# Block 0's V rows in two PSUM banks from the last recall on, and GpSimd for the lower parts of the weights from there

## The chip, the cores and the metric

The kernel runs on one core of a Trainium2 chip. The metric is the device time of one execution in microseconds (us). The engines are named as the profile names them: PE (TensorE matmul), PEld (its weight load), DVE (VectorE), ACT (ScalarE), POOL (GpSimd) and SP (SyncE, which issues most DMAs).

## The reference

One decoder layer on 512 tokens of width 1024. Three token mixers (forgetting attention, a sliding window, attention over a memory) each have a projection; sigmoid gates merge them and an output projection adds the sum to `x`. Then 8 heads choose 16 of 16384 one-neuron experts per token, so each token has 128 rows of `u` and 128 rows of `v`.

```
h = RMSNorm(x);  z = h @ w_in                     # q, k, v of the mixers, memory queries, three gates
merged = g0*(o_fox @ w_fox_o) + g1*(o_swa @ w_swa_o) + g2*(o_mem @ w_mem_o)
x = x + merged @ w_out
h2 = RMSNorm(x); experts, gates = top-16 per head by product keys
a = dot(h2, u[expert]);  x = x + sum_e gelu(a_e) * gate_e * v[expert_e]
```

## The kernel before

The 512 tokens are 4 blocks of 128 (one token per partition). `mixers(g, hT)` runs twice: for group 0 (block 0 alone) and for group 1 (blocks 1, 2 and 3 together, 384 tokens). Blocks 0 and 1 fetch their expert rows with GpSimd's indirect DMAs, one row of 1024 floats per token and expert; blocks 2 and 3 later multiply with all experts densely.

**Weights in two parts.** Matmuls are made exact by splitting: `load` (from L115) fetches a tile of 128 x 1024 into `raw` (SP's queue), ACT casts it into `whi` (L119), and `rest` (L122) makes the lower part `wlo = raw - whi`. `rest` adds its argument `pool` to a counter `due`; when that reaches 1, GpSimd makes this lower part (L129), else VectorE does (L131). `load_split` passes `share[0]` unless told otherwise. `raw`, `whi` and `wlo` have three buffers each. `mm3` (L145 to L147) multiplies three times per pair of parts, and two of the three need only `whi`.

**Rows beside the mixers.** While group 1 mixes, a generator `beside` works for block 0: the search for its experts, their choice, and then the rows. `pump` is called at each weight tile and each attention head, adds credit and lets the generator run. `step` (from L858) issues the gathers up to four rows ahead (L868, five buffers `row`) and uses the next one: a U row with a multiply that sums (L883, into `acts`), a V row with a multiply-add. As long as the list `two` is empty, a V row of block 0 is added to `x1[0]`, a tile `mg` in SBUF (L890: row, factor, `mg` in, `mg` out). Once `two` holds a tile of two PSUM banks, the first row of a block starts that sum (L893) and each further row is added to it there (L896). After a block's last row, `two` is added to `x1`. A step with `apart` goes another way: ACT scales the row (L886) and GpSimd adds it to `x1` in SBUF (L887). `beside` stops when 183 of block 0's 256 rows are done (128 U rows and 55 V rows).

**The end of group 1's mixers.** After the last `recall` (attention over the memory, L555 to L577, which sums in the bank `acc`) come `gates(1, 2)` with 8 weight tiles, `branch(1, 2)` with 4 (L604 and L605 gate and merge each product), the split of `merged` (L661, L662) and the output projection with 8 weight tiles (L673 adds `x`). These 20 tiles, 128 x 1024 each, have their lower parts made at L131, since `beside` set `share[0]` to 0 when it came to the rows. Then the pool `mixed` (banks `tg` and `acc`) is closed, `two` is opened in its place (L961 and L962), `x1` is normalized and turned (L239), and the search for blocks 1 to 3 begins.

**What sets the order.** Up to that search the framework's scheduler orders each engine's instructions ahead of time, by a priority that is the order in the program; the rows are pushed back by 400 places (`high_priority(-LATER)`). The order on each engine is then fixed: an instruction that waits holds all behind it on its engine. The dense part after the search is ordered by hand.

Of the kernel before, what the change touches and what calls it, by code (L numbers as in the profile page):

```python
# [7 lines left out]
F32 = mybir.dt.float32  # L8
# [8 lines left out]
S, D, NB, KC = 512, 1024, 4, 8  # L17
# [5 lines left out]
NJ = PH * TOPK  # L23
# [34 lines left out]
def tile_block(ctx: ExitStack, tc: tile.TileContext, t: dict, out: bass.AP):  # L58
# [12 lines left out]
    mixing, two = ExitStack(), []  # L71
    mixed = mixing.enter_context(tc.tile_pool(name="mixed", bufs=1, space=bass.MemoryType.PSUM))

    def bank(tag):
        return (mixed if BANKS[tag] == 1 else psum).tile([128, 512], F32, tag=tag, name=tag, bufs=BANKS[tag])
# [4 lines left out]
    def pump(part=1.0):  # L80
        if inside[0]:
            return
        inside[0] = True
        credit[0] += part * PACE[pace[0]]
        while credit[0] > 0:
            if pace[0] == "search":
                cost = next(side[0], None)
            else:
                with tc.high_priority(-LATER):
                    cost = next(side[0], None)  # L90
            if cost is None:
                credit[0] = 0.0
                break
            credit[0] -= cost
        inside[0] = False


    due, share = [0.0], [0.0]
# [50 lines left out]
    def small_f(n, tag, bufs=None):  # L149
        return small.tile([128, n], F32, tag=tag, name=tag, **({"bufs": bufs} if bufs else {}))  # L150
# [9 lines left out]
    def by_k(x):  # L160
        return x.rearrange("p (k s) -> p k s", k=KC)
# [156 lines left out]
    def halves(two):  # L318

        return two[:, :, :512], two[:, :, 512:]  # L320

    def gemm_tr(h, src):

        w = load_split(src, 8, 128)
        ps = bank("mm")[:, :h[0][0].shape[1]]
        for dc in range(KC):
            mm3(ps, (w[0][:, dc], w[1][:, dc]), (h[0][dc], h[1][dc]), dc == 0, dc == KC - 1)
        return ps
# [41 lines left out]
    def p_t(p, tiles):  # L370
        ps = bank("tp")
        for i in range(tiles):
            PE.transpose(ps[:, i * 128:(i + 1) * 128], p[:, i * 128:(i + 1) * 128], ident)
        pT = pp.tile([128, 512], F32, tag="pT", name="pT")
        A.copy(pT[:, :tiles * 128], ps[:, :tiles * 128])
        return pT

    def new_p():
        return pp.tile([128, 512], F32, tag="p", name="p")
# [5 lines left out]
    def finish(oT, po, den, nh, hd, i0, lb):  # L385

        w = nh * hd
        V.reciprocal(den, den)
        o = pp.tile([128, 512], F32, tag="o", name="o", bufs=1)
        V.tensor_mul(o[:, :w].rearrange("p (h d) -> p h d", h=nh), po[:, :w].rearrange("p (h d) -> p h d", h=nh),  # L390
                     den[:, :, None].to_broadcast([128, nh, hd]))
        ps = bank("tp")
        for i in range(w // 128):
            PE.transpose(ps[:, i * 128:(i + 1) * 128], o[:, i * 128:(i + 1) * 128], ident)
        dst = slice(i0, i0 + w // 128), slice(lb * 128, (lb + 1) * 128)
        split(oT[0][:, dst[0], dst[1]], oT[1][:, dst[0], dst[1]], ps[:, :w].rearrange("p (u t) -> p u t", t=128))
# [158 lines left out]
    def recall(g, qT, oT):  # L555
        for lb in range(len(GROUPS[g])):
            po, den = bank("acc"), small_f(4, "fden")
            for i in range(2):
                pump(0.5)
                sc = bank("sc").rearrange("p (g k) -> p g k", g=2)  # L560
                nm, p = small_f(2, "nm"), new_p()
                for j in range(2):
                    PE.matmul(sc[:, j], qT[:, 2 * i + j, lb * 128:(lb + 1) * 128], mkT[:, 2 * i + j, :],
                              start=True, stop=True)
                V.tensor_reduce(nm, sc, axis=AX.X, op=OP.max, negate=True)
                for j in range(2):
                    A.activation(p[:, j * 256:(j + 1) * 256], sc[:, j], AF.Exp, bias=nm[:, j:j + 1],
                                 accum_out=den[:, 2 * i + j:2 * i + j + 1])
                pT = p_t(p, 4)
                for j in range(2):  # L570
                    h = 2 * i + j
                    for k in range(2):
                        PE.matmul(po[:, h * 128:(h + 1) * 128], pT[:, (2 * j + k) * 128:(2 * j + k + 1) * 128],
                                  mv[:, k, h * 128:(h + 1) * 128], start=k == 0, stop=k == 1)
            finish(oT, po, den, 4, 128, 0, lb)


    def new_g(w):
        return pp.tile([128, BIG * 128], F32, tag="g", name="g", bufs=KC)[:, :w]

    def gates(g, i, hT, ccs=range(4)):
        gs = []
        for cc in ccs:
            c0 = 8 * i + 2 * cc
            if len(GROUPS[g]) == 1:
                bias = pp.tile([128, 256], F32, tag="sq", name="bias")
                for c in range(2):
                    A.activation(bias[:, c * 128:(c + 1) * 128], ident, AF.Copy, scale=hb[:, c0 + c:c0 + c + 1])
                gs.append(new_g(256))
                gemm_nat(hT, halves(t["w_tr"][c0:c0 + 2]), 256, 1,  # L590
                         lambda b, ps: A.activation(gs[-1], ps, AF.Tanh, scale=0.5), more=bias)
                continue
            for c in range(2):
                ps = gemm_tr(hT, t["w_tr"][c0 + c])
                gs.append(new_g(ps.shape[1]))
                A.activation(gs[-1], ps, AF.Tanh, bias=hbh[:, c0 + c:c0 + c + 1], scale=0.5)
        return gs

    def branch(grp, i, merged, oT, gs):
# [7 lines left out]
        for cc in range(4):  # L607
# [7 lines left out]
            for c in range(2):  # L615
# [4 lines left out]
                        kc == 0, kc == 3)  # L620
                gated(by_k(merged)[:, 2 * cc + c], gs[2 * cc + c], ps)

    def mixers(g, hT):

        nb = len(GROUPS[g])
        skvf(g, hT)
        oT = new_oT(g)
        qT = fox_qkv(g, 0, hT)
        if g == 0:
            memory()  # L630
            biases()
        fox(g, 0, qT, oT)
        qT = fox_qkv(g, 1, hT)
        fox(g, 1, qT, oT)
        merged = wide(f"mg{g}", nb)
        gs = gates(g, 0, hT)
        qT = window_q(g, hT)
        branch(g, 0, merged, oT, gs)
        oT = new_oT(g)
        window(g, qT, oT)  # L640
        gs = gates(g, 1, hT)
        qT = memory_q(g, hT)
        branch(g, 1, merged, oT, gs)
        oT = new_oT(g)
        recall(g, qT, oT)
        gs = gates(g, 2, hT)
        if g == 0:
            get_x()
        branch(g, 2, merged, oT, gs)

        mT = [by_k(ep.tile([128, D], F32, tag="own", name="own"))] if nb == 1 else pair(nb)
        if nb == 1:
            for q in range(2):
                ps = bank("tp")
                for i in range(4):
                    PE.transpose(ps[:, i * 128:(i + 1) * 128], merged[:, (4 * q + i) * 128:(4 * q + i + 1) * 128], ident)
                ps, dst = ps.rearrange("p (k s) -> p k s", k=4), slice(4 * q, 4 * q + 4)
                A.activation(mT[0][:, dst], ps, AF.Copy, scale=0.5)
        else:
            for ct, src in enumerate(chunks(by_k(merged))):  # L660
                A.activation(mT[0][:, ct], src, AF.Copy, scale=0.5)  # L661
                V.scalar_tensor_tensor(mT[1][:, ct], src, 0.5, mT[0][:, ct].bitcast(F32),  # L662
                                       op0=OP.mult, op1=OP.subtract)
        mT = [chunks(x) for x in mT]
        x1, sums = by_token(wide(f"mg{g}", nb)), new_sums(4)
        for c in range(4):
            xs = [new_g(256) for _ in range(nb)]
            cols = slice(c * 256, c * 256 + 256)
            for lb, b in enumerate(GROUPS[g]):
                nc.sync.dma_start(xs[lb], t["x"][b * 128:(b + 1) * 128, cols])  # L670

            def use(b, ps):
                V.tensor_add(x1[:, b, cols], xs[b], ps)  # L673
                squares(x1[:, b, cols], sums[:, b, c:c + 1])

            if nb == 1:
                gemm_plain(mT[0], t["w_out"][c], 256, use, load_raw)
            else:
                gemm_nat(mT, t["w_out"][c], 256, nb, use)
        return x1, sums  # L680
# [174 lines left out]
    known, issued, done, ahead, flying, rpool = [2 * NJ], [0], [0], [AHEAD], {}, []  # L855
# [102 lines left out]
    share[0] = 0.5  # L958
    xb, sums = mixers(1, hT)
    side[0] = iter(())  # L960
    mixing.close()  # L961
    two.append(ctx.enter_context(tc.tile_pool(name="two", bufs=1, space=bass.MemoryType.PSUM)).tile([128, D], F32, name="two"))  # L962
    for lb, b in enumerate(GROUPS[1]):
        x1[b] = xb[:, lb]
    pre.close()
# [390 lines left out]
```

## Time and profile before

| what | value |
|---|---|
| median of 3 runs | 1589.84 us (1589.75 to 5559.83) |
| profiled execution, its own time | 1593.83 us |
| its span in the profile | 1592.1 us |
| mean granted TensorE clock | 0.982 |
| busy share: PE, PEld, DVE, ACT, POOL | 95, 86, 90, 52, 49 % |

The profile shows one execution. Its page gives busy time per engine and groups of instructions by line; further views of the same trace give the groups of one stretch, what an engine waited for, the chain of work that ended last, and the instructions in order of time. PE is the engine with the largest share, but a share is a mean over stages, so a stage has to be looked at by itself. The time of the profiled execution is 4.0 us above the median.

### The profile page before, as it was taken

The numbers are of one execution on the slowest core, as the hardware profiler recorded it, in microseconds if no ns is written. First come the engines' busy times: TensorE is split into PE (matmuls) and PEld (weight loads), VectorE is DVE, ScalarE is ACT, GpSimd is POOL, SyncE is SP. The second block draws the span as 40 slices with busy tenths as digits, with TensorE's granted clock in tenths as the row PEclk, the third lists the DMA queues.
The fourth block names the chain that finished last, engine by engine and source line by source line (L and its number), as shares of the span: only waits on it lengthen the run. The fifth ranks groups of instructions, "written<-read, shape, count | busy, mean of one in ns | idle before, by whom it ended". The sixth has DMA issues, their size and how long they took to land.

```text
span 1592.1 us, 27209 instructions
## 1 busy us (share of the span) xinstructions
PE 1514.5 (95%) x9458; PEld 1374.6 (86%) x9458; DVE 1433.5 (90%) x2666; ACT 829.5 (52%) x1840; POOL 779.0 (49%) x639
## 2 busy tenths in 40 slices
PE   8999899999999989999995999899999999999998
PEld 7989799997888988999885898788888888888887
DVE  6678477989899999999899999799999999999998
ACT  7778336646345534454215998554454444454443
POOL 1100015768576455467744665455555454555451
PEclk9999999999999999999997999999999999999999
DMA  8677657898899899965897999999999999999995
GB/s 328 222 236 249 242 182 247 316 357 299 314 346 322 273 348 346 382 217 185 290 411 247 380 393 392 344 399 390 409 410 410 409 411 409 395 409 411 410 409 213
DMA packets 178361, 531.90 MB, mean 334 GB/s; under 512 B 17456, under 2 KB 46384, under 8 KB 178224
## 3 DMA queue, kind: packets, MB, share of 16 engines
q0 software_dynamic: 73728, 268.47, 44.8%
q1 hardware_dynamic: 94416, 225.95, 38.9%
q10 hardware_dynamic: 10080, 35.75, 5.6%
q8 instruction: 74, 1.21, 0.3%
q14 instruction: 63, 0.52, 0.1%
HBM read 515.42 MB, written 14.68 MB: 333 GB/s over the span
## 4 chain that ended last, share of the span: by engine, by line
PE 54%; DVE 13%; issue 12%; DMA 11%; POOL 6%; ACT 4%; DVEq 0%; POOLq 0%; SPq 0%; ACTq 0%
PE mm L146 8%; PE mm L1029 8%; PE mm L147 8%; PE mm L145 8%; DMA row<-in_peer_v_dram,eidx 5%; POOL row L868 4%; DMA row<-in_peer_u_dram,eidx 4%; DVE wlo L131 3%; PE sc L1103 3%; DVE two L896 2%; PE sc L146 1%; PE sc L147 1%; PE sc L145 1%; PE tp L145 1%; PE tp L146 1%
## 5 line engine op out<-in xcount | busy, mean ns | idle before, releaser
L868 POOL DMA_INDIRECT row<-in_peer_v_dram,eidx x256 | 320.9, 1254 | 287.1 <-DVE two L896 162.8
L868 POOL DMA_INDIRECT row<-in_peer_u_dram,eidx x256 | 318.2, 1243 | 237.2 <-DVE scr L883 135.0
L131 DVE TENSOR_TENSOR wlo<-raw,whi 128x1024 fp32r<-128x1024 f32 (+1 forms) x244 | 304.2, 1248 | 33.6 <-ACT whi L119 26.5
L896 DVE SCALAR_TENSOR_TENSOR two<-row,acts,two 128x1024 f32<-128x1024 f32 x176 | 226.2, 1285 | 3.4 <-DMA row<-in_peer_v_dram,eidx 1.1
L119 ACT CAST whi<-raw 128x1024 fp32r<-128x1024 f32 x146 | 152.6, 1050 | 100.4 <-PE mm L146 62.4
L883 DVE SCALAR_TENSOR_TENSOR scr<-row,own 128x1024 bf16<-128x1024 f32 x128 | 156.3, 1221 | 22.2 <-DMA row<-in_peer_u_dram,eidx 21.2
L883 DVE SCALAR_TENSOR_TENSOR scr<-row,two 128x1024 bf16<-128x1024 f32 x117 | 142.2, 1216 | 6.0 <-DMA row<-in_peer_u_dram,eidx 5.0
L203 POOL TENSOR_TENSOR rsy<-rsv,mhalf 128x4 f32<-128x4 f32 (+5 forms) x25 | 39.9, 1600 | 184.3 <-DVE rsv L202 130.5
L1156 ACT CAST ah<-ga 128x256 fp32r<-128x256 f32 x116 | 47.1, 407 | 156.3 <-PE tp L146 118.4
L145 PE MATMUL mm<-hhi,whi 128*128 128x384 f32 x320 | 110.1, 344 | 1.2 <-DVE mg L673 0.7
L1158 ACT CAST whi<-raw 128x1024 fp32r<-128x1024 f32 x96 | 100.4, 1048 | 18.2 <-DMA raw<-in_peer_v_dram 12.7
L146 PE MATMUL mm<-hlo,whi 128*128 128x384 f32 x320 | 109.7, 343 | 0.0
L147 PE MATMUL mm<-hhi,wlo 128*128 128x384 f32 x320 | 108.9, 340 | 0.0
L146 PE MATMUL sc<-wlo,ah 128*128 128x512 f32 x256 | 101.4, 396 | 6.3 <-DVE wlo L131 6.3
L145 PE MATMUL mm<-whi,hhi 128*128 128x256 f32 (+1 forms) x360 | 103.7, 290 | 2.9 <-DVE g L604 1.9
L146 PE MATMUL mm<-wlo,hhi 128*128 128x256 f32 (+1 forms) x360 | 102.6, 286 | 1.7 <-DVE wlo L131 1.6
L147 PE MATMUL mm<-whi,hlo 128*128 128x256 f32 (+1 forms) x360 | 101.9, 285 | 0.8 <-DVE hlo L662 0.8
L147 PE MATMUL sc<-whi,al 128*128 128x512 f32 x256 | 101.8, 398 | 0.0
L145 PE MATMUL sc<-whi,ah 128*128 128x512 f32 x256 | 101.3, 396 | 0.2 <-ACT whi L1158 0.2
L145 PE MATMUL tp<-whi,ah 128*128 128x512 f32 x256 | 101.1, 395 | 0.0
L146 PE MATMUL tp<-wlo,ah 128*128 128x512 f32 x256 | 100.8, 394 | 0.0
L147 PE MATMUL tp<-whi,al 128*128 128x512 f32 x256 | 100.7, 393 | 0.0
(322 smaller groups left out, 4544.9 us busy)
## 6 DMA issues: line engine op xcount, KB each, us to landing
raw<-in_peer_v_dram SPq DMA_DIRECT2D x96, 512.0 KB
hhi<-in_uT_dram ACTq DMA_DIRECT2D x68, 512.0 KB
raw<-in_w_tr_dram SPq DMA_DIRECT2D x48, 512.0 KB
raw<-in_w_nat_dram SPq DMA_DIRECT2D x40, 512.0 KB
last<-in_peer_v_dram SPq DMA_DIRECT2D x32, 512.0 KB
hhi<-in_uT_dram SPq DMA_DIRECT2D x26, 512.0 KB
raw<-in_w_o_dram SPq DMA_DIRECT2D x24, 512.0 KB
gd<-st SPq DMA_DIRECT2D x24, 512.0 KB
```

The source lines that it names most:

```text
L119: (cast or A.copy)(hi[:, :n * w], raw[:, :n * w])
L131: V.tensor_sub(lo, raw, hi.bitcast(F32))
L145: PE.matmul(ps, lh, rh, start=first, stop=False)
L146: PE.matmul(ps, lh, rl, start=False, stop=False)
L147: PE.matmul(ps, ll, rh, start=False, stop=last)
L868: G.indirect_dma_start(out=r, out_offset=None, in_=t["peer_" + tab], in_offset=bass.IndirectOffsetOnAxis(ap=eidx[b][:, j:j + 1], axis=0))
L883: V.scalar_tensor_tensor(scr, r, 1.0, two[0] if b else h2n[b], op0=OP.mult, op1=OP.mult, accum_out=acts[b][:, c]))
L896: V.scalar_tensor_tensor(two[0], r, acts[b][:, c], two[0], op0=OP.mult, op1=OP.add))
L1029: PE.matmul(ps[:, :TD], w[:, dc], h2f[dc], start=dc == 0, stop=dc == KC - 1)
L1103: PE.matmul(ps[:, u], o[:, 1, u], o[:, 0, u], start=True, stop=True)
L1156: A.copy(ah, a)
L1158: A.copy(hi, raw)
```

## The change

`rows_in_psum` is new: it closes the pool `mixed`, opens the two banks as `two` and sets `share[0]` to 1, so that each later `load_split` of group 1's mixers hands its lower part to GpSimd. `mixers` calls it for group 1 right after the last `recall`. The two lines that closed `mixed` and opened `two` after the mixers are gone. `share[0]` goes back to 0 ahead of the last search, as before. From L623 on line numbers are up to 9 higher in the changed kernel (L868 is L877, L890 is L899, L893 is L902, L896 is L905).

```diff
+    def rows_in_psum():
+        mixing.close()
+        pool = ctx.enter_context(tc.tile_pool(name="two", bufs=1, space=bass.MemoryType.PSUM))
+        two.append(pool.tile([128, D], F32, name="two"))
+        assert done[0] >= NJ
+        share[0] = 1.0
+
     def mixers(g, hT):
...
         oT = new_oT(g)
         recall(g, qT, oT)
+        if g:
+            rows_in_psum()
         gs = gates(g, 2, hT)
...
     side[0] = iter(())
-    mixing.close()
-    two.append(ctx.enter_context(tc.tile_pool(name="two", bufs=1, space=bass.MemoryType.PSUM)).tile([128, D], F32, name="two"))
```

Two places show how the built orders differ. The first is POOL's order from the first V row's gather on, the stretch in which the 20 lower parts are needed (`row` is a row buffer, `eidx` the chosen experts, `wlo` a lower part). Before:

```order
L868 DMA row<-in_peer_u_dram,eidx_206 128x1024 x6
L868 DMA row<-in_peer_v_dram,eidx_206 128x1024 x52
L203 TENSOR_TENSOR rsy<-rsv,mhalf 128x3
L868 DMA row<-in_peer_v_dram,eidx_206 128x1024 x6
L722 TENSOR_TENSOR cand<-v_7904 128x3x24
```

Now, the start of the same stretch:

```order
L877 DMA row<-in_peer_v_dram,eidx_206 128x1024
L129 TENSOR_TENSOR wlo<-raw,whi 128x1024
L877 DMA row<-in_peer_v_dram,eidx_206 128x1024 x3
L129 TENSOR_TENSOR wlo<-raw,whi 128x1024
L877 DMA row<-in_peer_v_dram,eidx_206 128x1024 x2
L129 TENSOR_TENSOR wlo<-raw,whi 128x1024
L877 DMA row<-in_peer_v_dram,eidx_206 128x1024 x3
L129 TENSOR_TENSOR wlo<-raw,whi 128x1024
```

So it goes on for all 20: one to four gathers stand ahead of each lower part, 45 gathers from the first lower part to the last.

The second place is DVE's order where `x1` is turned, at the end of the mixers (`mg_2288` is `x1[0]` in SBUF, `hlo<-tp` the turn of `x1`). Before:

```order
L239 SCALAR_TENSOR_TENSOR hlo<-sc,gcol,hhi 128x384
L890 SCALAR_TENSOR_TENSOR mg_2288<-row,acts_207,mg_2288 128x1024
L1044 COPY rstd<-rsy 128x3
L890 SCALAR_TENSOR_TENSOR mg_2288<-row,acts_207,mg_2288 128x1024
L131 TENSOR_TENSOR wlo<-raw,whi 128x1024
```

Now:

```order
L239 SCALAR_TENSOR_TENSOR hlo<-sc,gcol,hhi 128x384
L902 TENSOR_SCALAR two<-row,acts_207 128x1024
L899 SCALAR_TENSOR_TENSOR mg_2288<-row,acts_207,mg_2288 128x1024
L1051 COPY rstd<-rsy 128x3
L905 SCALAR_TENSOR_TENSOR two<-row,acts_207,two 128x1024
```

The first row that goes to `two` stands behind the last lower part of this stage, and behind the turn of `x1`: the rows run about 400 places late. Of the 55 early V rows 49 still go to `mg` in SBUF and 6 to `two`. From the dense part on PE's, POOL's and SP's orders are as before.

## The prediction

> **What bounds the kernel now.** I first read the page (span, busy shares, the chain), then the busy time by stage, since the change touches one stage only.
>
> ```profile
> span 1592.1 us, 27209 instructions
> PE 1514.5 (95%) x9458; PEld 1374.6 (86%) x9458; DVE 1433.5 (90%) x2666; ACT 829.5 (52%) x1840; POOL 779.0 (49%) x639
> ```
>
> PE is busy in 95% of the span, so time can only be won where PE idles. The stretches below are the last recall with all 20 lower parts up to the first turn of `x1` (L239), the start of the search, its rest, and the first dense part.
>
> ```profile
> core 0: us, PE busy (x) PEld busy (x) DVE busy (x) ACT busy (x) POOL busy (x), PEclk, DMA share, GB/s
> 519.80:637.20 117.40, 108.99 (x734) 106.06 (x732) 112.04 (x137) 50.91 (x97) 63.81 (x48) 1.00 0.90 322
> 637.20:676.00 38.80, 36.97 (x232) 36.39 (x233) 38.34 (x125) 16.63 (x32) 18.05 (x18) 1.00 0.99 383
> 676.00:760.00 84.00, 83.48 (x463) 78.41 (x462) 78.73 (x490) 41.86 (x62) 58.29 (x55) 1.00 0.59 205
> 760.00:836.00 76.00, 74.47 (x346) 65.03 (x344) 74.08 (x109) 11.53 (x27) 46.93 (x40) 1.00 0.93 356
> ```
>
> In the first stretch, 117.40 us long, PE idles 117.40 - 108.99 = 8.4 us, DVE only 5.4 us, and POOL 53.6 us. DVE is the tightest engine beside PE: it sets PE's gaps, and POOL looks free. What a change here adds or saves reaches the end: behind it PE idles 1.8 us of 38.8, 0.5 of 84 and 1.5 of 76, and the orders there are nearly as before, so there is little slack to swallow a delay. What DVE does in the stretch, by group:
>
> ```profile
> L890 DVE SCALAR_TENSOR_TENSOR mg<-row,acts,mg 128x1024 f32<-128x1024 f32 x45 | 57.7, 1283 | 3.0 <-DMA row<-in_peer_v_dram,eidx 2.2 <-DVE mg L673 0.5
> L131 DVE TENSOR_TENSOR wlo<-raw,whi 128x1024 fp32r<-128x1024 f32 x22 | 26.8, 1220 | 1.6 <-ACT whi L119 0.8 <-issue 0.8
> L605 DVE TENSOR_TENSOR mg<-mg,g 128x384 f32<-128x384 f32 x14 | 7.6, 549 | 0.0
> L883 DVE SCALAR_TENSOR_TENSOR scr<-row,own 128x1024 bf16<-128x1024 f32 x4 | 4.9, 1217 | 0.0
> L662 DVE SCALAR_TENSOR_TENSOR hlo<-mg,hhi 128x384 fp32r<-128x384 f32 x8 | 4.3, 555 | 0.0
> ```
>
> And all that POOL does there, with what it waited for:
>
> ```profile
> L868 POOL DMA_INDIRECT row<-in_peer_v_dram,eidx x48 | 63.8, 1329 | 53.3 <-DVE mg L890 35.2 <-DVE scr L883 6.1 <-DVE fden L388 4.7
> ```
>
> POOL's 53 idle us are mostly waits for DVE to give back a row buffer: it is paced by the rows.
>
> **The change part by part.** *Removed:* 20 of these lower parts leave DVE, 20 x 1.220 = 24.4 us. DVE's busy time in the stretch falls from 112.0 to 87.6 us.
>
> *Added:* 20 subtractions of 128 x 1024 on POOL. The trace has none there; the nearest row is POOL's addition of a row to `mg`, of the same shape, type and number of inputs.
>
> ```profile
> L887 POOL TENSOR_TENSOR mg<-mg,row x23: 2353/2367/2420, 676.4 to 895.2; 128x1024 f32<-128x1024 f32 x23
> ```
>
> 20 x 2.367 = 47.3 us. POOL's work becomes 63.8 + 47.3 = 111.1 us of 117.4. It is no longer free.
>
> *The V rows in PSUM.* The row's own price does not change: 1285 ns against 1283.
>
> ```profile
> L896 DVE SCALAR_TENSOR_TENSOR two<-row,acts,two 128x1024 f32<-128x1024 f32 x176 | 226.2, 1285 | 3.4 <-DMA row<-in_peer_v_dram,eidx 1.1
> ```
>
> By the built order, 49 of the 55 early V rows still go to `mg` in SBUF, and the first one to `two` stands behind the turn of `x1`, later than all 20 lower parts. So this half of the change costs and saves nothing in the stretch (0, at most a few tenths for 6 rows). [...]
>
> *A new conflict between DVE and POOL.* In the search stage POOL's L887 and DVE's L131, which both read two SBUF tiles, already meet. POOL first, then DVE in the same stretch (start, duration):
>
> ```profile
> 679.27 1.13 POOL L722 TENSOR_TENSOR cand<-v 128x24 f32<-128x24 f32 x1 [0.49 <-DVE v L714]
> 681.52 2.40 POOL L887 TENSOR_TENSOR mg<-mg,row 128x1024 f32<-128x1024 f32 x1
> 683.86 1.27 POOL L722 TENSOR_TENSOR cand<-v 128x48 f32<-128x48 f32 x1
> ```
>
> ```profile
> 679.09 1.22 DVE L131 TENSOR_TENSOR wlo<-raw,whi 128x1024 fp32r<-128x1024 f32 x1
> 681.94 3.08 DVE L131 TENSOR_TENSOR wlo<-raw,whi 128x1024 fp32r<-128x1024 f32 x1
> ```
>
> The L131 that starts at 681.94 inside POOL's addition (681.52 to 683.92) ends at 685.02: 1.10 us after POOL's, about its own length. It did nothing until POOL was done. The other way round, POOL's small `cand` at 679.27 ends at 680.40, 0.09 us after the L131 of 679.09, though such a one can take 0.23 us. They exclude each other and take turns. Over the stage:
>
> ```profile
> L131 DVE TENSOR_TENSOR wlo<-raw,whi x7: 1197/1977/3709, 679.1 to 726.0; 128x1024 fp32r<-128x1024 f32 x7
> L131 DVE TENSOR_TENSOR wlo<-raw,whi x22: 1217/1220/1226, 521.9 to 634.6; 128x1024 fp32r<-128x1024 f32 x22
> ```
>
> L131 takes 1977 ns at the median beside POOL's additions and 1220 in the stretch where POOL only gathers. [...]
>
> So I sum what excludes each other in the stretch. On DVE: rows 57.7, L605 7.6, U rows 4.9, L662 4.3, and the two lower parts that stay there 2.4 = 76.9 us. On POOL 47.3. Together **124.2 us** in a stretch of 117.4: **+6.8 us** if they follow one another without a gap. That is the lower bound of a loss.
>
> *POOL's own queue.* It is in order, and ahead of each lower part stand one to four gathers that wait for row buffers. Two rows of POOL (start, duration, idle before) show the gap between gathers that wait for nothing:
>
> ```profile
> 544.68 1.01 POOL L868 DMA_INDIRECT row<-in_peer_v_dram,eidx  x1 [0.31 <-issue]
> 546.00 1.38 POOL L868 DMA_INDIRECT row<-in_peer_v_dram,eidx  x1 [0.30 <-issue]
> ```
>
> 0.3 us for each of 48 gathers is 14.4: 111.1 + 14.4 = 125.5 us, **+8.1**. Each subtraction may also have to wait for a DVE instruction that is under way, on average half of 1.28, 0.6 us: 20 x 0.6 = 12 more, 137.5 us, **+20.1**. That is the upper bound of the likeliest case. Since part of these waits falls in time that a gather would have waited anyway, I take a third of the 12: 8.1 + 4 = **+12**. PE loses it as waits for `wlo`, and DVE as rows that last longer.
>
> *Hidden at first.* DVE starts the first of these lower parts at 521.88, while PE uses it only at 534.41:
>
> ```profile
> 521.88 1.22 DVE L131 TENSOR_TENSOR wlo<-raw,whi 128x1024 fp32r<-128x1024 f32 x1
> 534.41 0.42 PE L145 MATMUL mm<-hhi,whi 128*128 128x384 f32 x1
> ```
>
> This lead of 12.5 us covers a late `wlo` in the gates. It does not shorten the stretch: its last instructions on DVE wait for the rows ahead of them, and these for the gathers on POOL. Where the lead is gone, `raw`, `whi` and `wlo` (three buffers each) are given back late too, and SP's loads come later. The opening of `two` costs nothing: its banks were last read by the last recall, and by the built order the first write to them comes behind the first turn of `x1`, at 637.20 in the trace of before.
>
> **Sum:** in the profiled execution 1592.1 + 12 = 1604.1 us of span (1605.8 with what lies around it, as 1593.83 to 1592.1 now). The median of the runs is 4.0 us below the profiled execution's time, so I predict 1589.84 + 12 = **1601.8 us**. The likeliest case alone spans +6 to +20: 1596 to 1610.
>
> **Rivals.** *A, a gain.* In gates and branches the lead of 12.5 us holds, and 24.4 us less on DVE close PE's gaps that DVE made. For it speaks how slowly PE asks for lower parts while it still fills its time, one in 5.1 to 5.5 us:
>
> ```profile
> 545.33 1.23 DVE L131 TENSOR_TENSOR wlo<-raw,whi 128x1024 fp32r<-128x1024 f32 x1 [0.46 <-ACT whi L119]
> 550.44 1.22 DVE L131 TENSOR_TENSOR wlo<-raw,whi 128x1024 fp32r<-128x1024 f32 x1 [0.77 <-issue]
> 555.89 1.22 DVE L131 TENSOR_TENSOR wlo<-raw,whi 128x1024 fp32r<-128x1024 f32 x1
> ```
>
> A decides as soon as POOL's round per tile is shorter than that. POOL's round is 2.37 + 45/20 gathers x (1.33 + 0.3) = 6.0 us; with gathers at 0.95 and hidden gaps it is 4.5. Then PE gets back up to its 8.4 idle us: 1582 to 1586. Against it: the sum of 124.2 us. Chance 0.17.
>
> *B, no change.* Relief and conflict cancel: DVE's 24.4 us less are spent waiting for POOL's 47.3, of which half meets DVE instructions that do not read two SBUF tiles. 1586 to 1594. For it: rows are filler, 400 places late, and may stretch without PE noticing. Chance 0.20.
>
> *C, POOL as the bound from end to end.* Gathers beside DVE's two-input work often take 1.69 to 1.88 us (mean 1.33, because some ran undisturbed); if all 48 took 1.7, POOL's sum is 48 x (1.7 + 0.3) + 47.3 = 143 us, and with 12 us of waits 155: +26 to +38, 1616 to 1628. Against it: DVE's and POOL's turns leave gaps in which a gather is short. Chance 0.13, of which 0.03 beyond 2%.
>
> *That the change doesn't do what it says* is half true by the order (6 rows of 55 in PSUM); the lower parts are on POOL for certain, 20 in the built order.
>
> **How the numbers follow.** Likeliest 0.50, A 0.17, B 0.20, C 0.13. A measurement of this kernel tells about 2% (31.8 us) from no change. Faster by over 2% would need four times PE's idle time of this stretch: 0.01. Slower by over 2% is the end of C: 0.03. Within 2%: 0.96. The range runs from the middle of A to the start of C, 1584 to 1616 us.
>
> **What would show it.** In the changed profile: 20 subtractions at L129 on POOL of about 2.4 us each. The V rows into `mg` (L899) last longer than 1283 ns, 1.6 to 1.9 us in the mean, and L605 and the split of `merged` (L671) over 0.55. PE waits for `wlo` of L129 at the end of the gates and in the output projection. From 519.8 the first turn at L239 comes about 129 us later instead of 117. Behind it all durations are as before. Wrong would be: rows at 1283 ns although POOL subtracts beside them (then the exclusion doesn't hold here, and A or B follow); PE without waits for `wlo` and still a longer stretch (then DVE's order, not POOL's queue, sets it); or a delay that is given back after 760 us.

## The result, and the profile after

| what | before | changed |
|---|---|---|
| median of the runs | 1589.84 us | 1614.28 us (1613.19 to 1615.74, 5 runs) |
| ratio to before, 95% interval | | 1.0138 [1.0117, 1.0159] |
| profiled execution: its own time, its span | 1593.83, 1592.1 us | 1613.19, 1611.1 us |
| the stretch from the fourth-last U row of block 0 to the first turn of `x1` (L239) | 117.4 us | 141.6 us |

One execution of the kernel before took 5559.83 us; the ratio leaves it out. The change costs about 24 us by the medians (22 by the ratio, 19 to 25 by its interval). All of it lies in the one stretch of the prediction: 141.6 - 117.4 = **24.2 us**. (The two spans differ by 19.0 only because the profiled execution of before had already lost some 4 us ahead of this stretch.)

The first view is the busy time by stage of the changed kernel, with the same four stages as in the prediction: length, busy time of PE, PEld, DVE, ACT and POOL with their counts, granted clock of PE, DMA share, GB/s.

```profile
core 0: us, PE busy (x) PEld busy (x) DVE busy (x) ACT busy (x) POOL busy (x), PEclk, DMA share, GB/s
515.40:656.95 141.55, 118.76 (x733) 112.76 (x731) 127.58 (x118) 49.43 (x97) 113.06 (x70) 0.94 0.80 270
656.95:695.80 38.85, 37.53 (x233) 36.88 (x234) 38.41 (x133) 18.20 (x32) 16.55 (x18) 1.00 1.00 375
695.80:779.00 83.20, 83.00 (x464) 78.27 (x464) 77.89 (x481) 40.95 (x62) 55.16 (x55) 1.00 0.59 204
779.00:855.00 76.00, 74.34 (x345) 64.96 (x343) 73.31 (x108) 11.63 (x27) 46.81 (x40) 1.00 0.92 354
```

The three later stages last as long as before (38.85, 83.2 and 76.0 us against 38.8, 84.0 and 76.0), so nothing is given back. In the first, DVE issues fewer instructions (118 instead of 137) and is yet busy 127.6 us instead of 112.0. The groups of that stretch, of DVE and then of POOL (busy us, mean ns of one, idle time before), show how:

```profile
L899 DVE SCALAR_TENSOR_TENSOR mg<-row,acts,mg 128x1024 f32<-128x1024 f32 x46 | 87.0, 1891 | 10.7 <-DMA row<-in_peer_v_dram,eidx 10.0
L605 DVE TENSOR_TENSOR mg<-mg,g 128x384 f32<-128x384 f32 x14 | 10.8, 779 | 0.0
L892 DVE SCALAR_TENSOR_TENSOR scr<-row,own 128x1024 bf16<-128x1024 f32 x4 | 7.4, 1840 | 0.0
L604 DVE SCALAR_TENSOR_TENSOR g<-g,mm 128x384 f32<-128x384 f32 x13 | 7.1, 542 | 0.0
L671 DVE SCALAR_TENSOR_TENSOR hlo<-mg,hhi 128x384 fp32r<-128x384 f32 x8 | 7.0, 882 | 0.0
L682 DVE TENSOR_TENSOR mg<-g,mm 128x256 f32<-128x256 f32 x12 | 4.9, 412 | 3.3 <-PE mm L147 3.3
L131 DVE TENSOR_TENSOR wlo<-raw,whi 128x1024 fp32r<-128x1024 f32 x2 | 2.4, 1216 | 0.0
```

```profile
L877 POOL DMA_INDIRECT row<-in_peer_v_dram,eidx x50 | 63.6, 1272 | 27.2 <-DVE mg L899 15.5 <-issue 6.6 <-DVE scr L892 1.4
L129 POOL TENSOR_TENSOR wlo<-raw,whi 128x1024 fp32r<-128x1024 f32 x20 | 50.2, 2511 | 1.5 <-ACT whi L119 1.1
```

Four DVE groups with two SBUF inputs have grown: the rows (L899) from 1283 to 1891 ns, L605 from 549 to 779, the U rows (L892) from 1217 to 1840, the split of `merged` (L671) from 555 to 882. L604, of the same shape as L605 and with one of its inputs in PSUM, takes 542 ns (548 before). The two lower parts that stay on DVE (L131) have two SBUF inputs too and take 1216 ns (1220 before); they start at 650.00 and 655.50, behind the last of POOL's subtractions, which ends at 648.98. POOL is not full: its groups leave 28 of 141.6 us idle.

**DVE's account.** Without the 20 lower parts DVE would be busy 87.6 us. It is busy 127.6: 1.3 of the 40.0 us more are one row more in the stretch, and the 38.7 us that remain I take for time in which an instruction has begun and stands still. The growth of the four groups, added up from their rows, is 36.4 us; the records of neighbouring instructions overlap a little, so that the two ways differ. That is 1.8 to 1.9 us for each subtraction on POOL, which saved DVE 1.22. DVE's idle time goes from 5.4 to 14.0 us, 10.0 of it waits for gathered rows (2.2 before). So -24.4 + 38.7 + 1.3 + 8.6 = **24.2 us**. This closes by construction, since the 38.7 are a remainder; it says where DVE's time went, not what caused what.

What PE waits for in the stretch (in total, times, longest):

```profile
PE mm L145 <- DVE g L604: 10.0, 7, 2.1
PE mm L147 <- POOL wlo L129: 2.8, 2, 1.7
PE mm L146 <- POOL wlo L129: 2.8, 2, 2.4
PE mm L147 <- DVE hlo L671: 2.2, 2, 1.5
```

Only 5.6 us are waits for POOL's lower parts. The largest is for DVE's gating at L604, which sets a bank `mm` free (10.0 us, 3.2 before). One such case, DVE, POOL and PE in turn (start, duration, what):

```profile
586.71 3.47 DVE L899 SCALAR_TENSOR_TENSOR mg<-row,acts,mg 128x1024 f32<-128x1024 f32 x1
590.10 0.54 DVE L605 TENSOR_TENSOR mg<-mg,g 128x384 f32<-128x384 f32 x1
590.57 0.54 DVE L604 SCALAR_TENSOR_TENSOR g<-g,mm 128x384 f32<-128x384 f32 x1
```

```profile
586.69 2.40 POOL L129 TENSOR_TENSOR wlo<-raw,whi 128x1024 fp32r<-128x1024 f32 x1
589.24 1.77 POOL L877 DMA_INDIRECT row<-in_peer_v_dram,eidx  x1 [0.16 <-issue]
```

```profile
588.86 0.33 PE L147 MATMUL mm<-ohi,wlo 128*128 128x384 f32 x1
591.16 0.69 PE L145 MATMUL mm<-ohi,whi 128*128 128x384 f32 x1 [1.97 <-DVE g L604]
591.65 0.52 PE L146 MATMUL mm<-olo,whi 128*128 128x384 f32 x1
```

POOL's subtraction begins 0.02 us ahead of the row at 586.71. The row ends at 590.18, 1.09 us after POOL's end at 589.09, and lasts 3.47 instead of 1.28. Behind it in DVE's fixed order stand L605 and L604, and PE stands still for 1.97 us until L604 has read its bank. Then its matmuls, 0.33 to 0.34 us before, last 0.52: the granted clock has fallen to half, of which more at the end.

### The profile page after: what moved, and what is told of

It reads as the page before. It is cut to its first block, busy times and chain, and to the rows that moved or that the text cites. A ratio compares the mean times of both kernels' runs of the same rounds, so it can differ in the third digit from the quotient of the medians.

```text
span 1611.1 us, 27218 instructions
## 1 busy us (share of the span) xinstructions
PE 1519.1 (94%) x9458; PEld 1377.8 (86%) x9458; DVE 1447.5 (90%) x2646; ACT 828.7 (51%) x1840; POOL 829.9 (52%) x659
## 3 DMA queue, kind: packets, MB, share of 16 engines
q8 instruction: 74, 1.21, 0.3%
## 4 chain that ended last, share of the span: by engine, by line
PE 53%; DVE 15%; issue 13%; DMA 8%; POOL 8%; ACT 3%; another core or an unknown queue 0%; POOLq 0%; DVEq 0%; SPq 0%; ACTq 0%
PE mm L1036 9%; PE mm L146 8%; PE mm L147 8%; PE mm L145 7%; POOL row L877 5%; DMA row<-in_peer_v_dram,eidx 4%; DVE wlo L131 3%; PE sc L1110 3%; DVE two L905 2%; DMA row<-in_peer_u_dram,eidx 2%; PE sc L147 2%; PE sc L146 2%; PE tp L145 2%; PE tp L146 2%; PE sc L145 2%
## 5 line engine op out<-in xcount | busy, mean ns | idle before, releaser
L877 POOL DMA_INDIRECT row<-in_peer_v_dram,eidx x256 | 319.6, 1249 | 263.0 <-DVE two L905 161.0
L877 POOL DMA_INDIRECT row<-in_peer_u_dram,eidx x256 | 324.1, 1266 | 228.1 <-DVE scr L892 119.9
L131 DVE TENSOR_TENSOR wlo<-raw,whi 128x1024 fp32r<-128x1024 f32 (+1 forms) x224 | 279.9, 1252 | 28.3 <-ACT whi L119 25.6
L905 DVE SCALAR_TENSOR_TENSOR two<-row,acts,two 128x1024 f32<-128x1024 f32 x182 | 233.7, 1284 | 4.0 <-DMA row<-in_peer_v_dram,eidx 1.8
L892 DVE SCALAR_TENSOR_TENSOR scr<-row,own 128x1024 bf16<-128x1024 f32 x128 | 158.7, 1240 | 20.1 <-DMA row<-in_peer_u_dram,eidx 18.9
L892 DVE SCALAR_TENSOR_TENSOR scr<-row,two 128x1024 bf16<-128x1024 f32 x117 | 142.2, 1215 | 4.4 <-DMA row<-in_peer_u_dram,eidx 2.6
L147 PE MATMUL mm<-hhi,wlo 128*128 128x384 f32 x320 | 109.0, 341 | 0.0
```

What stands on the lines that cost most here:

```text
L131: V.tensor_sub(lo, raw, hi.bitcast(F32))
L147: PE.matmul(ps, ll, rh, start=False, stop=last)
L877: G.indirect_dma_start(out=r, out_offset=None, in_=t["peer_" + tab], in_offset=bass.IndirectOffsetOnAxis(ap=eidx[b][:, j:j + 1], axis=0))
L892: V.scalar_tensor_tensor(scr, r, 1.0, two[0] if b else h2n[b], op0=OP.mult, op1=OP.mult, accum_out=acts[b][:, c]))
L905: V.scalar_tensor_tensor(two[0], r, acts[b][:, c], two[0], op0=OP.mult, op1=OP.add))
```

## The experiments

Line numbers of the experiments differ by a few from those of the changed kernel; the names of the tiles tell the instructions apart. The last column is the length of the stretch in the profiled execution. The experiments ran on three chips, each with its own runs of the kernel before (medians 1588.5, 1589.2 and 1586.2 us); each ratio is to the runs on the same chip.

| run | what | median us | ratio to before, 95% | stretch us |
|---|---|---|---|---|
| psum_alone | PSUM half of the change | 1588.44 | 1.0001 [0.9978, 1.0024] | 118.5 |
| pool_alone | GpSimd half | 1613.72 | 1.0165 [1.0148, 1.0182] | 141.9 |
| half_pool | 10 of 20 on GpSimd | 1598.37 | 1.0071 [1.0044, 1.0098] | 128.6 |
| gates_pool | the gates' 8 alone | 1600.48 | 1.0073 [1.0044, 1.0102] | 133.2 |
| nogather_only | without gathers | 1584.18 | 0.9988 [0.9975, 1.0001] | 116.7 |
| nogather_pool | the same, 20 on GpSimd | 1609.42 | 1.0156 [1.0124, 1.0188] | 144.6 |
| reduce_only | rows read one tile | 1593.99 | 1.0027 [1.0009, 1.0045] | 124.8 |
| reduce_pool | the same, 20 on GpSimd | 1603.94 | 1.0088 [1.0053, 1.0124] | 129.9 |
| bank_only | rows summed in PSUM | 1609.23 | 1.0124 [1.0107, 1.0141] | 143.8 |
| bank_pool | the same, 20 on GpSimd | 1609.21 | 1.0143 [1.0115, 1.0172] | 141.5 |
| ahead3_only | gathers 3 ahead | 1585.95 | 1.0001 [0.9983, 1.0020] | 118.3 |
| ahead3_pool | the same, with the change | 1612.83 | 1.0162 [1.0134, 1.0191] | 142.1 |

### Which half of the change costs: psum_alone and pool_alone

The first takes the share out of the change:

```diff
         assert done[0] >= NJ
-        share[0] = 1.0
```

The second is the kernel before with the share alone:

```diff
         recall(g, qT, oT)
+        if g:
+            share[0] = 1.0
         gs = gates(g, 2, hT)
```

> The two PSUM banks are opened after the last recall as in the change, but share stays 0, so VectorE makes all 20 lower parts as before. Theory (VectorE's instructions with two SBUF inputs and GpSimd's subtractions exclude each other; the opening of the banks does nothing): 1590 us, within 3 us of before, stretch 117 us, V rows into mg 1.28 us in the mean. Rival 'the early opening and the other order cost the time': 1600 to 1614 us.

> The lower parts go to GpSimd after the last recall, but the two banks are opened after the mixers as before. Theory of exclusion: all of the loss is here, 1611 to 1617 us, V rows into mg 1.85 to 1.95 us in the mean. Rival 'GpSimd's queue is late': the same, 1611 to 1617 us. Rival 'the opening of the banks costs': 1590 to 1600 us.

The PSUM half does nothing (1.0001), the GpSimd half costs all (1.0165). With the PSUM half alone the early rows into `mg` are as in before; with the GpSimd half alone they are as in the changed kernel. The V rows' group of each, from 430 to 660 us:

```profile
L898 DVE SCALAR_TENSOR_TENSOR mg<-row,acts,mg 128x1024 f32<-128x1024 f32 x49 | 62.7, 1280 | 2.0 <-DMA row<-in_peer_v_dram,eidx 1.5 <-issue 0.2
```

```profile
L892 DVE SCALAR_TENSOR_TENSOR mg<-row,acts,mg 128x1024 f32<-128x1024 f32 x47 | 89.6, 1907 | 9.8 <-DMA row<-in_peer_v_dram,eidx 9.1
```

So the early opening of the banks and the other order that it brings are out as causes.

### How much GpSimd work, and where: half_pool and gates_pool

`half_pool` is pool_alone with `share[0] = 0.5`. `gates_pool` is the change with one more edit:

```diff
         gs = gates(g, 2, hT)
+        if g:
+            share[0] = 0.0
```

> Share 0.5 after the last recall: 10 of the 20 lower parts on GpSimd, 10 on VectorE; the banks are opened after the mixers. Theory of exclusion: each subtraction on GpSimd keeps VectorE out for 2.0 us and saves it 1.22, whatever else GpSimd does, so about half of the loss: + 9 to + 15 us, 1598 to 1605. Rival 'GpSimd's queue is late': its work is 64 + 24 + 14 us of gaps = 102 of 117, it is not full, so no loss: 1586 to 1593 us.

> The change, but share goes back to 0 after the gates: only the 8 lower parts of the gates are on GpSimd, the 12 of the branch and of the output projection are VectorE's. Theory of exclusion: 8/20 of the loss, + 8 to + 12 us, 1597 to 1602. Rival 'TensorE gets wlo late': the gates run 12 us ahead of need, so nothing is lost there: 1586 to 1592 us, and the loss belongs to the branch and the output projection.

Ten subtractions cost 0.0071 x 1589 = 11.3 us (7 to 16 by the interval), inside the 9 to 15 of the exclusion. GpSimd is idle 42 of 128.6 us there, and the loss has not gone, as it should have by the rival:

```profile
L870 POOL DMA_INDIRECT row<-in_peer_v_dram,eidx x52 | 60.8, 1170 | 39.5 <-DVE mg L892 28.5 <-issue 5.6 <-DVE scr L885 2.3
L129 POOL TENSOR_TENSOR wlo<-raw,whi 128x1024 fp32r<-128x1024 f32 x10 | 26.0, 2602 | 3.0 <-ACT whi L119 2.3 <-issue 0.5
```

The eight of the gates alone cost 0.0073 x 1589 = 11.6 us (7 to 16 by the interval), at the upper end of the 8 to 12 expected; in the profiled execution the stretch grew by more, 15.8 us. The lead of `wlo` over its use in the gates saves nothing, so it is not late lower parts that cost.

### GpSimd without its gathers: nogather_only and nogather_pool

Both kernels (before, and the change) leave out the gathers of the early V rows but the first, and add that row each time:

```diff
             b, tab, j = JOBS[n]
+            if NJ < n < EARLY_ROWS:
+                flying[n] = flying[NJ] if n == NJ + 1 else flying[n - 1]
+                continue
```

> Left out: all gathers of early V rows but the first; VectorE adds the same row again each time, with its own factor and two SBUF inputs. VectorE makes all lower parts, as before. It is the base for nogather_pool: rows never wait for a gather, and GpSimd is all but empty. 1578 to 1592 us under every theory (the DMA queues carry less, waits for rows were only 2 us).

> The change, with those gathers left out as well: GpSimd has only its 20 subtractions, so neither gaps between gathers nor late rows remain, and only the exclusion does. Exclusion alone as the whole cause: nogather_only + 20 to + 26 us. Two causes, exclusion and rows that come late because their gathers stand behind subtractions in GpSimd's queue: nogather_only + 8 to + 17. GpSimd's queue as the whole cause: nogather_only - 4 to + 4.

The difference is 25.2 us by the medians, as large as that of the change, and inside the 20 to 26 expected of the exclusion alone. Late gathers cannot be the reason here. This is all it does in the stretch, and DVE's rows beside it:

```profile
L129 POOL TENSOR_TENSOR wlo<-raw,whi 128x1024 fp32r<-128x1024 f32 x20 | 53.3, 2668 | 68.9 <-ACT whi L119 68.9
L880 POOL DMA_INDIRECT row<-in_peer_v_dram,eidx x5 | 5.1, 1010 | 9.5 <-DVE mg L902 5.7 <-DVE scr L895 1.4 <-DVE fden L388 1.2
```

```profile
L902 DVE SCALAR_TENSOR_TENSOR mg<-row,acts,mg 128x1024 f32<-128x1024 f32 x49 | 91.5, 1868 | 0.8
L908 DVE SCALAR_TENSOR_TENSOR two<-row,acts,two 128x1024 f32<-128x1024 f32 x5 | 6.4, 1276 | 0.0
```

POOL waits 69 us for ACT's `whi`: each subtraction starts as soon as it can. DVE never waits for a row. And yet the rows take 1868 ns where they read `mg`, and 1276 where they read PSUM. That fits the exclusion as the whole cause, with one reservation. Without gathers the scheduler's order is another one: 54 rows stand in the stretch instead of 45, 9 x 1.28 = 11.5 us more of DVE's time. How much of the 25.2 us these cost can't be read from this pair. What it does show is that the rows are held up by subtractions alone. That the exclusion makes the whole loss without a late gather fits the pair, but is not shown by it.

### Rows that read one tile: reduce_only and reduce_pool

```diff
-                V.scalar_tensor_tensor(x1[b], r, acts[b][:, c], x1[b], op0=OP.mult, op1=OP.add))
+                V.tensor_reduce(x1[b][:, c], r, axis=AX.X, op=OP.add))
```

This leaves the sum of the early V rows out, in before and in the change.

> Left out: the early V rows of block 0 are not added to mg; in place of the multiply-add, VectorE sums the row into one column of mg (one SBUF input, no factor). VectorE makes all lower parts, as before. It is the base for reduce_pool. All theories: the load of VectorE is about the same (a reduction of 512 elements took 0.68 us, so one of 1024 some 1.2 to 1.3), 1582 to 1594 us.

> The change, with the same rows as reduce_only (one SBUF input; the sum of the early V rows is left out). Banks and stages are those of the change. Theory of exclusion: the early rows last as long as in reduce_only though GpSimd subtracts beside them; of the 24 us at most 6 stay (L605, L671 and the U rows still read two tiles), reduce_only - 6 to + 6. Rival 'GpSimd's queue is late': gathers, gaps and subtractions on GpSimd are the same as in the change, so reduce_only + 12 to + 24 us.

The rows and the rest of DVE, and POOL, in the stretch of reduce_pool:

```profile
L899 DVE TENSOR_REDUCE mg<-row 128x1 f32<-128x1024 f32 x49 | 58.8, 1210 | 13.9 <-DMA row<-in_peer_v_dram,eidx 13.6
L605 DVE TENSOR_TENSOR mg<-mg,g 128x384 f32<-128x384 f32 x14 | 13.3, 961 | 0.0
L671 DVE SCALAR_TENSOR_TENSOR hlo<-mg,hhi 128x384 fp32r<-128x384 f32 x8 | 8.2, 1036 | 0.0
```

```profile
L877 POOL DMA_INDIRECT row<-in_peer_v_dram,eidx x52 | 51.1, 982 | 22.7 <-DVE mg L899 9.0 <-issue 7.5 <-DVE scr L892 2.4
L129 POOL TENSOR_TENSOR wlo<-raw,whi 128x1024 fp32r<-128x1024 f32 x20 | 48.6, 2430 | 5.9 <-ACT whi L119 4.6 <-issue 1.0
```

The rows, which read one SBUF tile, take 1210 ns, as in reduce_only (1211), though 20 subtractions of 2.43 us run beside them. Of the loss of 24 us, 10.0 are left by the medians (1 to 18 by the two intervals), 5.1 by the stretches. By the medians the expectation of neither theory holds: 10 is above the 6 of the exclusion and below the 12 of the queue; the intervals reach into both. The pair has a flaw like the one before: reduce_only has 55 rows in its stretch and reduce_pool 49, 6 x 1.21 = 7.3 us less of DVE's time, so up to that much more of a loss may be hidden. Two things can be read of what is left. L605 and L671 still read two tiles and last longer than in before, 14 x 0.41 + 8 x 0.48 = 9.6 us. And DVE, with less to do, now waits 13.6 us for rows, of which some have their gathers behind subtractions on POOL, and 8.7 us for PE at L682.

### Rows summed in PSUM from the first: bank_only and bank_pool

Both open the banks before the second branch's gates, with the transposes of the memory branch in `tp` alone and the last recall's sum in `mm`. `rows_in_psum` stands in both without its share, and only bank_pool sets the share:

```diff
+        if g:
+            rows_in_psum()
         gs = gates(g, 1, hT)
...
         recall(g, qT, oT)
+        if g:
+            share[0] = 1.0
...
-            ps = bank(("tg", "tp")[n % 2])
+            ps = bank("tp" if two else ("tg", "tp")[n % 2])
...
-            po, den = bank("acc"), small_f(4, "fden")
+            po, den = bank("mm" if two else "acc"), small_f(4, "fden")
```

> The two banks are opened ahead of the gates of the second branch (the memory branch's transposes then use the bank tp alone, and the last recall sums in mm), so that all early V rows but one are summed in PSUM. VectorE makes all lower parts. It is the base for bank_pool. All theories: rows 1.28 us as in mg, 1587 to 1597 us; up to 5 us may go to the shared banks.

> As bank_only, and GpSimd makes the 20 lower parts after the last recall: the V rows in the stretch now read one SBUF tile only. Theory of exclusion: rows last 1.28 us although GpSimd subtracts beside them, the 20 subtractions cost nothing or win something: 1580 to 1594 us, at most bank_only + 3. Rival 'GpSimd's queue is late': its 111 us of work and its gaps stay, so the loss stays: bank_only + 12 to + 24 us, 1600 to 1616 us, with waits of TensorE for wlo.

The rows behave as the exclusion says. In bank_pool:

```profile
L905 DVE SCALAR_TENSOR_TENSOR two<-row,acts,two 128x1024 f32<-128x1024 f32 x50 | 64.2, 1284 | 13.1 <-DMA row<-in_peer_v_dram,eidx 10.3 <-issue 2.0
L129 POOL TENSOR_TENSOR wlo<-raw,whi 128x1024 fp32r<-128x1024 f32 x20 | 48.8, 2441 | 7.7 <-ACT whi L119 6.7 <-issue 0.7
```

1284 ns, undisturbed, and GpSimd's lower parts cost nothing on top by the medians (1609.21 against 1609.23 us), 3 us by the ratios, with -4 to +10 by their intervals. But the base missed its expectation by far: bank_only itself is 20 us slower than before. Among TensorE's waits there, from 420 to 656 us, are 6.9 us for the recall's output at L390, against 1.0 before:

```profile
PE tp L394 <- DVE o L390: 6.9, 4, 2.9
```

A base with that much slack can hide a late queue, so that the zero difference is weaker evidence than the rows' 1284 ns. As a remedy it is worth nothing: with the two banks opened this early the kernel is as slow as with the exclusion.

### Gathers one row later: ahead3_only and ahead3_pool

```diff
-        while issued[0] < min(known[0], done[0] + ahead[0] + 1):
+        while issued[0] < min(known[0], done[0] + (3 if NJ <= done[0] < EARLY_ROWS else ahead[0]) + 1):
```

> The kernel before, but early V rows are gathered up to 3 rows ahead, not 4 (the instructions and their order on each engine stay the same). It is the base for ahead3_pool. VectorE waits only 2 us for rows now, and GpSimd issues each gather as soon as a buffer comes free: 1588 to 1596 us under every theory.

> The change, with early V rows gathered 3 ahead. Exclusion alone as the whole cause: as in the change, against ahead3_only + 22 to + 27 us. Two causes: a gather that starts one row later behind a subtraction of 2.4 us is late by up to a row more, so the waits for rows grow from 10 us, and the loss is ahead3_only + 28 to + 45.

The difference is 26.9 us, which is what the exclusion alone was to give, but the pair tells nothing: the edit did not change what it was to change. (ahead3_only, at 1585.95 us, lies below the 1588 expected, as the kernel before does on that chip.) POOL issues the gathers of the stretch in the same order, and its waits in ahead3_pool are those of the changed kernel, 15.5 us for L899 in both, as are DVE's for rows (9.8 against 10.0 us):

```profile
POOL row L877 <- DVE mg L899: 15.5, 13, 2.1
POOL row L877 <- issue: 6.6, 27, 0.3
```

What limits the gathers is the five buffers that DVE gives back, not the distance in the program, so none starts a row later. The pair stands as a second measurement of the change.

### What follows

Shown: the GpSimd half alone costs; the cost grows with the number of subtractions and begins in the gates; DVE's rows were held up by subtractions where they read two SBUF tiles (1891 ns in the changed kernel, 1907 in pool_alone, 1868 in nogather_pool with a GpSimd that does little else), and not where they read one (1284 in bank_pool, 1276 in nogather_pool, 1210 in reduce_pool); where the rows read one tile, 10 us of loss are left by the medians, with an interval that leaves it open whether that is less than half. Not shown by a run: how the 24 us divide between instructions that stand still and rows that come late, since each experiment that takes one away moves the other or the order of the rows. The next section gives what the two traces say of it. A run in which late gathers alone are taken away, with the rows in their places, was not made, and more row buffers were not tried.

## Why the prediction was right, and where not

The direction, the place and the mechanism were right; the size was half. The prediction gave +12 us, with +6 to +20 for its likeliest case; +24 came. That 1614.28 us still lies inside 1584 to 1616 is luck: the range reached so far only for the start of rival C, whose way of losing time did not come.

- *The PSUM half costs and saves nothing:* right (psum_alone 1.0001).
- *Removed, 24.4 us of DVE:* right. *Added, 20 x 2.367 = 47.3 us on POOL:* 50.2, 2511 ns in the mean: the six that began while a row on DVE had 0.47 to 0.77 us to go took 2700 to 3017 ns, the other 14 took 2347 to 2418.
- *The exclusion, "124.2 us in a stretch of 117.4: +6.8 us if they follow one another without a gap":* this is the step that failed. That the rows, L605, the U rows and L662 take turns with subtractions as L131 does was not shown there; the changed profile shows it by their 1891, 779, 1840 and 882 ns. The sum was right; what it was set against was not. By the start and end times in the two traces, a subtraction or a DVE instruction with two SBUF inputs is under way in 97.8 us of the stretch before and in 122.3 us now, 24.5 us more. The rest of the stretch, in which DVE works on one SBUF input or idles, stays: 19.6 us before, 19.2 now. The prediction compared 124.2 with the whole stretch, as if this rest would vanish beside the subtractions. But an instruction that stands still holds those behind it on DVE (the row of 586.71, for 3.47 us, held L605 and L604), and only 3.3 us of work with one SBUF input ran beside a subtraction. Set against the same DVE groups in its own view of before (57.7 + 26.8 + 7.6 + 4.9 + 4.3 = 101.3 us), the prediction's sum gives 124.2 - 101.3 = **+22.9 us**.
- *POOL's queue, "+8.1", and "a third of the 12":* the wrong engine was summed. POOL was idle 28 us and did not set the length. Late rows did come: DVE waited 10.0 us for rows instead of 2.2. But of its 14.0 idle us 6.7 lie beside subtractions, in time that the exclusion counts already; outside of them DVE idled 7.3 us, against 5.4 before. In this account of one execution of each kernel the late rows add 2 us at most, and the loss is the exclusion's.
- *"PE loses it as waits for `wlo`":* a small part, 5.6 us. 10.0 us are waits for L604, because gating stands behind the delayed rows in DVE's queue. The prediction had this as a sign of being wrong: "then DVE's order, not POOL's queue, sets it". That rows are "filler" (rival B) was the same error: a row that nobody waits for held those behind it.
- *The lead in the gates covers:* wrong for the reason above; gates_pool lost 11.6 us.
- *Behind it all as before:* right, 38.85, 83.2 and 76.0 us.
- Of the signs: 20 subtractions of 2.40 us at the median, rows of 1.89 us and L605 and L671 over 0.55 came as foretold; the first turn after 129 us came after 141.6.
- Rivals A and B needed DVE's saved time to reach PE; half_pool, where GpSimd had time to spare, still lost 11.3 us. C had the size (+26 and more) by another way: its gathers of 1.7 us took 1.27, and POOL was never full.

## What to carry to other kernels

Work moved from VectorE to GpSimd may not be off VectorE: here, where both read two SBUF tiles, each 1.22 us moved came back as 1.8 to 1.9 us of standing still. Sum the work that excludes each other and compare it with what the same work took before, not with the length of the stretch: the rest of VectorE's work and its idle time stayed here (19.6 and 19.2 us). Then see what stands behind such an instruction in its order: here a row that stood still in front of a gating that frees a bank cost TensorE a wait of 1.97 us. And look in the built order whether the part of the change that was to keep the two engines apart (rows in PSUM, 1284 ns beside subtractions in bank_pool) is there in time: 6 of 55 rows were.

## What the runs showed of the hardware

TensorE's granted clock fell to half after a short wait. Three pieces of the changed kernel around the wait above:

```profile
589.00:591.20 2.20, 0.23 (x3) 0.04 (x1) 2.20 (x4) 0.52 (x2) 1.85 (x2) 0.98 0.93 343
591.20:594.60 3.40, 3.40 (x11) 3.40 (x12) 3.40 (x3) 1.46 (x2) 3.26 (x2) 0.51 0.88 280
594.60:595.00 0.40, 0.40 (x3) 0.14 (x1) 0.40 (x1) 0.00 (x0) 0.40 (x1) 1.00 0.92 307
```

In 2.20 us PE was busy for 0.23; then the granted clock was 0.51 for 3.40 us, and 1.00 after that. Not each such wait did this. In before, where the clock was 1.00 in the whole stretch, PE had a gap of nearly the same length, 1.94 us:

```profile
595.93 0.36 PE L145 MATMUL mm<-whi,hhi 128*128 128x256 f32 x1 [1.94 <-DVE g L604]
```

In the changed kernel's stretch half clock began at 553.59, 591.13, 601.37, 618.44 and 638.92 us, each time for 3.41 us. These starts lie 11, 3, 5 and 6 times 3.41 us apart. PE was busy for 1.28, 1.47, 1.33, 1.75 and 0.99 us of the 3.41 us just ahead of them. In the 3.41 us of before that end with its gap PE was busy for 1.48 us, and the clock stayed at 1.00. So neither the length of a gap nor this share tells by itself whether the clock fell; what does is not shown.

In before the whole stretch ran at 1.00, in the changed kernel at 0.94. PE's idle time rose by 14.4 us, and its busy time by 9.8, from 109.0 to 118.8 us for the same matmuls. How much of the 9.8 us lengthened the stretch is not shown; DVE's waits for PE grew only from 0.7 to 3.3 us.
